# Hybrid encoder layer: v's second half as one 512-column panel, the backward scan's products on VectorE, the third chunk's attention factors behind the merge

## The chip, the cores and the metric

The kernel runs on one core of one Trainium2 chip. The metric is the device time of one execution in microseconds (us). Engines are named as in the profile: PE (TensorE, matmuls), PEld (its weight loads), DVE (VectorE), ACT (ScalarE), POOL (GpSimd) and SP (SyncE), whose queue issues the kernel's loads and stores. L12 is line 12 of the kernel.

## The reference

One encoder layer, in float32, over a prompt of 512 tokens and a sample of 1024 tokens, 1024 channels each. Both go through the same weights:

```python
h = rmsnorm(x, norm_pre_mix) @ w_in          # q, k, v, z, xBC, dt, gates
att = diff_attention(q, k, v, lam, rel_bias) # 8 heads of 2 x 64, v of 128
att = rmsnorm(att, subln_w) * (1 - LAM_INIT) # per head, over its 128 channels
ssm = ssd_scan(forward) + ssd_scan(backward) # 16 heads of 64, chunks of 128
m = gate_a * (att @ w_proj_attn) + gate_s * (ssm @ w_proj_ssm)
x = x + rmsnorm(m @ w_out, norm_post_mix)
y = x + rmsnorm(swiglu(rmsnorm(x, norm_pre_ffn)), norm_post_ffn)
```

(Names are shortened here; the bodies matter only as far as told below.) The attention's bias comes from a table of 32 distance buckets for each head. The scan keeps, for every chunk of 128 tokens and each of two groups, a state of 128 x 512 that is multiplied by a decay and to which a product of b with the weighted x is added; the backward scan does this from the last chunk to the first.

## The kernel before

**Products.** Each float32 operand is split into a high and a low part (`split`: a cast, then a subtraction), and each product is three matmuls (L169, L170, L171). All 1536 tokens are held as `hT`, in three chunks of 512 columns. A weight panel is 1024 rows by 256 columns: two raw pieces `wraw` of 512 KB are loaded (L156), cast to `whi` by ACT (L137) and subtracted to `wlo` by DVE (L138). `wraw`, `whi` and `wlo` have two buffers each, so one panel can be prepared while the other is used.

**Order.** The program is recorded in the order in which it is written; a scheduler then sets one fixed order for every engine. Each engine runs its own order from first to last and waits where an operand or a buffer isn't ready. So does SP, whose order holds all transfers.

**v.** The first 512 columns of v are made in the loop that makes `hT`. The second 512 are made by `proj_tm` (called at L494) in two panels of 256 columns. For each, six pairs of 128-token tiles share one PSUM bank: 48 matmuls of 256 columns, then one DVE copy of 128x2x256 (L376) and one store to `v_d` (L377).

**The bias table.** Ahead of that, in a pool named `pre2`, four matmuls (`fb_ps`, L478) pick the bias for 2048 distances and 8 heads; ACT copies them to `fb` (L479), and a store (L480) puts `fb` into `f_d`. Then `skew(h)` (L485) copies, for each head, the row of `f_d` 128 times into `sk_d`, each row one element further: one transfer of 1 MB for each head, from memory to memory. `skew` names a DVE copy of v behind which the scheduler should put it; it is a hint on order, and the transfer doesn't wait for that copy. The attention loads `tb` from `sk_d` (L225).

**The backward scan** (L693 to L707) runs over the chunks from last to first and two groups, prompt and sample apart. In a step, PE makes `yo_ps` from the old state (L703), DVE makes `yb` from it (L705) and it is stored; `state_step` (L675) makes `xw` from x on POOL (L679), PE makes `st_ps` (L681), POOL multiplies the old state by `dec` (L686) and DVE adds `st_ps` (L687). The first state of a sequence is copied by DVE (L684), and its last chunk ends without a new state. PE's matmuls of the z projection stand between these steps. The forward scan calls `state_step` too.

**The heads and what follows.** A head's output `av` (128 channels by 512 tokens) is copied by ACT (L323) and stored to `att_d` (L324). `mean_square` squares `av` in place (L327), and PE sums it (`ms`, L330). When all heads of a chunk are done, `att_scale(c)` makes the factors of 8 heads x 512 tokens (`zq`, `msq`, `att_r`, some 16 small DVE operations to L342), transposes them (`rt`, L344) and stores them to `r_d` (L347). `att(c)` later loads, for each head, the rows of `att_d` (L352) and the factors from `r_d` (L353), multiplies (L354) and splits them into `big`. `merge(c)` projects these and makes the gated sum, `out_proj` multiplies it by w_out, `norms` does the two RMSNorms around the residual and transposes the result. Their order in the text is att(1), merge(1), norms(0), att(2), out_proj of the first sample chunk, merge(2), norms(1).

Of the kernel before, what the change touches and what calls it, by code (L numbers as in the profile page):

```python
# [18 lines left out]
P = 128  # L19
# [59 lines left out]
def hybrid_trunk_kernel(ctx: ExitStack, tc: tile.TileContext, a: dict, y_prompt, y_sample):  # L79
# [55 lines left out]
    def split(hi, lo, raw, eng=None):  # L135
        if eng == "act_dve":
            S.copy(hi, raw)  # L137
            V.tensor_sub(lo, raw, f(hi))  # L138
        elif eng == "pool_dve":
            G.tensor_scalar(hi, raw, 1.0, 0.0, op0=ALU.mult, op1=ALU.add)  # L140
            V.tensor_sub(lo, raw, f(hi))
        elif eng == "act_pool":
            S.copy(hi, raw)
            G.tensor_sub(lo, raw, f(hi))
        else:
            G.tensor_scalar(hi, raw, 1.0, 0.0, op0=ALU.mult, op1=ALU.add)
            G.tensor_sub(lo, raw, f(hi))
# [120 lines left out]
    def attention(base, SL, h, got, pend, zq, msq, qk, pp, at, qr, s_ps, t_ps, o_ps):  # L268
        nkb = SL // P
        tb = got["tb"]  # L270
        qh, ql, km = zip(got[0], got[1])
        v_h = at.tile([P, nkb, P], F32R, tag="vh", name="vh", bufs=1)
        v_l = at.tile([P, nkb, P], F32R, tag="vl", name="vl", bufs=1)
        raw = staged(qr, [P, nkb, P], (None, v_d[base:base + SL, h * P:(h + 1) * P].rearrange("(b p) e -> p b e", p=P)))
        split(v_h[:], v_l[:], raw[:])
        for qc in range(SL // 512):
            ops = o_ps.tile([P, 512], F32, tag="o", name="o")
            for q2 in range(2):
                aT = [at.tile([P, 2, 4, 256], F32R, tag=f"aT{b0}", name="aT", bufs=2 - b0 // 4)
                      for b0 in range(0, nkb, 4)]  # L280
                for u in range(2):
                    if pend and (q2, u) == ((0, 1) if qc and h == 7 else PU):
                        pend.pop()()
                        if qc and h == 7:
                            att_scale(1, zq[0], msq[0], ap, t_ps, "t")
                    qt = qc * 4 + q2 * 2 + u
                    qs = slice(qt * P, (qt + 1) * P)
                    off = P * (nkb - 1 - qt)
                    nm = pp.tile([P, 2], F32, tag="nm", name="nm")
                    zs = pp.tile([P, 2], F32, tag="zs", name="zs")  # L290
                    z0 = zq[qc][:, h, qt % 4:qt % 4 + 1]
                    pm = []
                    for m in range(2):
                        sps = s_ps.tile([P, SL], F32, tag="s", name="s")
                        for kc in range(0, SL, 512):
                            ks = slice(kc, kc + 512)
                            TE.matmul(sps[:, ks], qh[m][:, qs], km[m][:, ks], start=True, stop=False)
                            TE.matmul(sps[:, ks], ql[m][:, qs], km[m][:, ks], start=False, stop=True)  # L298
                        pt = pp.tile([P, SL], F32, tag=f"p{m}", name="pt", bufs=3)
                        V.tensor_tensor_reduce(out=pt[:], in0=sps[:], in1=tb[:, off:off + SL], scale=-1.0,  # L300
                                               scalar=3.0e38, op0=ALU.add, op1=ALU.min,
                                               accum_out=nm[:, m:m + 1])
                        S.activation(out=pt, in_=pt, func=AF.Exp, bias=nm[:, m:m + 1], scale=-1.0,  # L303
                                     accum_out=(z0, zs[:, 0:1])[m])
                        pm.append(pt)
                    V.reciprocal(zs[:, 0:1], zs[:, 0:1])
                    V.scalar_tensor_tensor(zs[:, 1:2], zs[:, 0:1], z0, neglam, op0=ALU.mult, op1=ALU.mult)
                    last_add.append(V.scalar_tensor_tensor(pm[0], pm[1], zs[:, 1:2], pm[0], op0=ALU.mult, op1=ALU.add))
                    for b0 in range(0, nkb, 4):
                        ps = t_ps.tile([P, 4, P], F32, tag="t", name="t")  # L310
                        for j in range(4):
                            TE.transpose(ps[:, j, :], pm[0][:, (b0 + j) * P:(b0 + j + 1) * P], ident)
                        us = slice(u * P, (u + 1) * P)
                        ab = aT[b0 // 4]
                        S.copy(ab[:, 0, :, us], ps)
                        V.tensor_sub(ab[:, 1, :, us], ps, f(ab[:, 0, :, us]))
                    if u == 0:
                        yield
                gemm(ops[:, q2 * 256:q2 * 256 + 256],
                     [(v_h[:, b, :], v_l[:, b, :], aT[b // 4][:, 0, b % 4, :], aT[b // 4][:, 1, b % 4, :]) for b in range(nkb)])  # L320
                yield
            av = pp.tile([P, 512], F32, tag="av", name="av", bufs=1)
            S.copy(av, ops)  # L323
            store(out=att_d[h * P:(h + 1) * P, base + qc * 512:base + qc * 512 + 512], in_=av)  # L324

            def mean_square(av=av, qc=qc):
                S.activation(out=av, in_=av, func=AF.Square)  # L327
                ps = t_ps.tile([P, 4, P], F32, tag="t", name="ms")
                for j in range(4):
                    TE.matmul(ps[:, 0, j:j + 1], av[:, j * P:(j + 1) * P], onec, start=True, stop=True)  # L330
                V.tensor_copy(msq[qc][:, h], ps[:, 0, 0:4])
            pend.append(mean_square)

    def att_scale(c, zq, msq, pool, psp, ptag):

# [25 lines left out]
    with ExitStack() as ph1:  # L361
# [12 lines left out]
        def evac_v(p0, t, ps):  # L374
            so = st0.tile([P, 2, 256], F32, tag="st0", name="st")
            done = V.tensor_copy(so, ps)  # L376
            store(out=v_d[t * P:(t + 2) * P, p0:p0 + 256].rearrange("(j p) n -> p j n", p=P), in_=so)  # L377
            return done
# [49 lines left out]
        def proj_tm(col0, ncol, evac, eng="act_dve", start=0):  # L428
            for p0 in range(start, ncol, 256):
                w = split_panel(w_in[:, col0 + p0:col0 + p0 + 256], eng=eng)  # L430
                for t in range(0, NT, 2):
                    ps = acc.tile([P, 2, 256], F32, tag="acc", name="acc")
                    for u in range(2):
                        tt = t + u
                        gemm_tm(ps[:, u, :], w, hT[tt // 4], slice((tt % 4) * P, (tt % 4 + 1) * P))
                    evac(p0, t, ps)
# [45 lines left out]
        def skew(h, after):  # L482
            dst = sk_d[h]
            with tc.issue_after(after.ins):
                store(out=bass.AP(tensor=dst.tensor, offset=dst.offset, ap=[[SKP + 1, P], [1, 2048]]),  # L485
                      in_=f_d[h:h + 1].broadcast_to([P, 2048]))

        def evac_v_skew(p0, t, ps):
            done = evac_v(p0, t, ps)
            n = (p0 - 512) // 256 * 6 + t // 2  # L490
            if n < 8:
                skew(n, done)

        proj_tm(V0, D, evac_v_skew, start=512)  # L494
        pools = [es.enter_context(tc.tile_pool(name="p" + n, bufs=b, reuse_waits="tile")) for n, b in (
            ("qk", 1), ("pp", 2), ("at", 1), ("qr", 2))]
        pools += [es.enter_context(tc.tile_pool(name="p" + n, bufs=b, space=PSUM, reuse_waits="tile")) for n, b in (
# [168 lines left out]
        def hb(tl, c, d_, g):  # L666
            return tl[:, c, d_ * 16 + g * 8:d_ * 16 + g * 8 + 8].unsqueeze(2).broadcast_to([P, 8, 64])

        def h3(ap):
            return ap.rearrange("p (h e) -> p h e", e=64)  # L670
# [4 lines left out]
        def state_step(c, d_, g, x_g, b_g, old, last):  # L675
            if last:
                return None
            xw = sc.tile([P, 512], F32, tag="xw", name="xw")
            G.tensor_mul(h3(xw[:]), h3(x_g), hb(wst, c, d_, g))  # L679
            ps = ssp.tile([P, 512], F32, tag="ssp", name="st_ps")  # L680
            TE.matmul(ps, b_g, xw, start=True, stop=True)  # L681
            new = sc.tile([P, 512], F32, tag=f"s{g}", name="state")
            if old is None:
                V.tensor_copy(new, ps)  # L684
            else:
                G.tensor_mul(h3(new[:]), h3(old[:]), hb(dec, c, d_, g))  # L686
                V.tensor_add(new, new, ps)  # L687
            return new

# [113 lines left out]
    with ExitStack() as ph2:  # L803
# [36 lines left out]
        def side_work():  # L840
# [49 lines left out]
        side = side_work()  # L890
        run(heads(512, 1024, range(8), pend, zq, msq, qk, pp, at, qr, s_ps, t_ps, o_ps),
            side, RATIO)
        pend.pop()()
        att_scale(2, zq[1], msq[1], ap, t_ps, "t")
        for _ in side:
            pass

# [1 line left out]
    with ExitStack() as ph3:  # L899
# [153 lines left out]
        with ExitStack() as ph3a:  # L1053
# [53 lines left out]
            for j, mt in enumerate(t0[0]):  # L1107
                load(out=mt, in_=mo_d[j * P:(j + 1) * P, :])
            m1 = merge(1, aT1)
            norms(0, t0)  # L1110
            aT2 = att(2)
            t1 = out_proj(m1)
# [130 lines left out]
```

## Time and profile before

| | us |
|---|---|
| median of 3 runs | 3193.4 (3191.82 to 3199.23) |
| profiled execution | 3186.2 |
| its span | 3184.4 |
| PE busy | 3029.6 |
| DVE busy | 1835.1 |
| ACT busy | 1260.8 |
| POOL busy | 651.3 |

The profile is of one execution. Busy times are sums over the span, so a high share says that an engine is seldom free, and not which stage is bound by it. Times on the trace are counted from the start of the span. On them the stages that the change touches stand here: v's second half from 101.7 to 175, the backward scan from 834 to 930, and the last head of the attention at 1864, behind which the first merge ends at about 1942 and the out projection after it at about 2004. The mean granted clock of PE is 0.98.

### The profile page before, as it was taken

What the parts mean: (1) busy time and instruction counts of PE and PEld (TensorE: products, weight loads), DVE (VectorE), ACT (ScalarE), POOL (GpSimd) and SP (SyncE); (2) the same over time, 40 slices, a digit from 0 to 9 for tenths busy, and PEclk for the clock granted to TensorE, in tenths of its full rate; (3) what the DMA queues carried; (4) which work ended last, traced back from release to release, by engine and by line L of the source; (5) the groups of instructions that cost most, each with busy time, mean ns of one, the idle gap of its engine ahead of it and who ended that gap; (6) DMA issues with size and microseconds to landing.
All of it is one profiled execution on the core that took longest, in us unless ns stands there. A gap on an engine that the chain in (4) does not pass through costs nothing. (4 is left out here: it accounts for less than half of the span.)

```text
span 3184.4 us, 44184 instructions
## 1 busy us (share of the span) xinstructions
PE 3029.6 (95%) x16668; PEld 2664.2 (84%) x16668; DVE 1835.1 (58%) x2974; ACT 1260.8 (40%) x2305; POOL 651.3 (20%) x508
## 2 busy tenths in 40 slices
PE   7999999999999999999998978978999999989998
PEld 7988887888887778788887867878999899978887
DVE  5214444455328995387877955686666766632444
ACT  4103333333303333366666734453333333332443
POOL 0001111000233442243232100023333433300000
PEclk9999999999999999999999989988999999999999
DMA  4633333223554445765544156644333333363454
GB/s 149 195 100 112 110 103 110 62 74 107 161 163 146 145 137 156 217 182 160 181 135 148 64 194 216 198 153 139 98 103 101 100 98 101 105 203 97 125 164 132
DMA packets 444238, 433.64 MB, mean 136 GB/s; under 512 B 25536, under 2 KB 360865, under 8 KB 442913
## 3 DMA queue, kind: packets, MB, share of 16 engines
q1 hardware_dynamic: 444025, 430.82, 43.5%
q8 instruction: 131, 2.15, 0.3%
q14 instruction: 82, 0.67, 0.1%
HBM read 316.58 MB, written 122.54 MB: 138 GB/s over the span
## 5 line engine op out<-in xcount | busy, mean ns | idle before, releaser
L169 PE MATMUL acc<-hT,whi 128*128 128x512 f32 x1056 | 421.3, 399 | 2.9 <-ACT st L455 2.9
L170 PE MATMUL acc<-hT,whi 128*128 128x512 f32 x1056 | 416.6, 395 | 0.0
L171 PE MATMUL acc<-hT,wlo 128*128 128x512 f32 x672 | 262.2, 390 | 0.0
L169 PEld LDWEIGHTS acc<-hT,whi 128*128 128x128 f32 x1056 | 198.9, 188 | 48.9 <-issue 5.5
L303 ACT ACTIVATE pt<-pt,nm 128x1024 f32<-128x1024 f32 (+1 forms) x192 | 193.1, 1007 | 116.2 <-DVE nm L300 113.1
L170 PEld LDWEIGHTS acc<-hT,whi 128*128 128x128 f32 x1056 | 199.0, 188 | 42.6 <-issue 3.6
L300 DVE CUSTOM_DVE_ANT_0 pt<-s,tb 128x1024 f32<-128x1024 f32 (+1 forms) x192 | 197.3, 1041 | 53.2 <-PE s L298 40.1
L169 PE MATMUL acc<-whi,hT 128*128 128x256 f32 x768 | 225.0, 293 | 0.6 <-ACT hT L208 0.4
L171 PE MATMUL acc<-whi,hT 128*128 128x256 f32 x768 | 224.7, 293 | 0.4 <-DVE hT L209 0.3
L170 PE MATMUL acc<-wlo,hT 128*128 128x256 f32 x768 | 224.0, 292 | 0.0
L169 PE MATMUL d<-dhi,fh 128*128 128x512 f32 x528 | 206.5, 391 | 5.9 <-ACT fh L137 5.9
L171 PE MATMUL d<-dhi,fl 128*128 128x512 f32 x528 | 206.3, 391 | 4.2 <-DVE fl L138 4.2
L170 PE MATMUL d<-dlo,fh 128*128 128x512 f32 x528 | 206.4, 391 | 0.0
L137 ACT CAST whi<-wraw 128x1024 fp32r<-128x1024 f32 (+1 forms) x115 | 115.8, 1036 | 216.4 <-PE acc L170 82.8
L138 DVE TENSOR_TENSOR fl<-raw,fh 128x896 fp32r<-128x896 f32 (+1 forms) x70 | 79.4, 1136 | 193.1 <-ACT fh L137 193.1
L169 PE MATMUL mm<-op,wy 128*128 128x384 f32 x528 | 178.9, 339 | 6.6 <-ACT op L137 5.0
L236 POOL TENSOR_TENSOR ql<-raw,qh 128x512 fp32r<-128x512 f32 x48 | 66.0, 1389 | 576.2 <-ACT qh L233 533.1
L170 PE MATMUL mm<-op,wy 128*128 128x384 f32 x528 | 178.6, 338 | 0.2 <-DVE op L138 0.2
L171 PE MATMUL mm<-op,wy 128*128 128x384 f32 x528 | 178.4, 338 | 0.0
L138 DVE TENSOR_TENSOR wlo<-wraw,whi 128x1024 fp32r<-128x1024 f32 x80 | 96.2, 1227 | 121.2 <-ACT whi L137 110.7
L169 PEld LDWEIGHTS acc<-whi,hT 128*128 128x128 f32 x768 | 148.0, 193 | 10.9 <-issue 9.4
L171 PE MATMUL acc<-hT,whi 128*128 128x512 f32 x384 | 155.5, 405 | 0.0
(375 smaller groups left out, 8191.1 us busy)
## 6 DMA issues: line engine op xcount, KB each, us to landing
wraw<-in_w_in_dram SPq DMA_DIRECT2D x60, 512.0 KB
wraw<-in_w_gate_up_dram SPq DMA_DIRECT2D x92, 256.0 KB
raw<-ff_d SPq DMA_DIRECT2D x46, 448.0 KB
wr<-in_w_gate_up_dram SPq DMA_DIRECT2D x80, 256.0 KB
ff_d<-c SPq DMA_DIRECT2D x88, 192.0 KB
g_d<-st SPq DMA_DIRECT2D x48, 256.0 KB
xg<-xs_d SPq DMA_DIRECT2D x48, 256.0 KB
gt<-g_d SPq DMA_DIRECT2D x48, 256.0 KB
```

The source lines that it names most:

```text
L137: S.copy(hi, raw)
L138: V.tensor_sub(lo, raw, f(hi))
L169: TE.matmul(ps, ah, bh, start=(i == 0), stop=False)
L170: TE.matmul(ps, ah, bl, start=False, stop=False)
L171: TE.matmul(ps, al, bh, start=False, stop=(i == n - 1))
L236: G.tensor_sub(q_l[:, s_], q_r[:, s_], f(q_h[:, s_]))
L300: V.tensor_tensor_reduce(out=pt[:], in0=sps[:], in1=tb[:, off:off + SL], scale=-1.0, scalar=3.0e38, op0=ALU.add, op1=ALU.min, accum_out=nm ...
L303: S.activation(out=pt, in_=pt, func=AF.Exp, bias=nm[:, m:m + 1], scale=-1.0, accum_out=(z0, zs[:, 0:1])[m])
```

## The change

Three edits. First, v's second half is one panel of 512 columns, in a pool `vp` with one buffer for each of `vhi` and `vlo`. Four raw pieces (two column halves by two row halves) are loaded and split into it; twelve tiles of 128 tokens follow, each 24 matmuls of 512 columns, a DVE copy and a store of 128x512. A skew is named behind each of the first eight. Second, in the backward scan `xw` and the state's product with `dec` go to DVE. Third, the last head's `mean_square` and the third chunk's `att_scale` are taken from the end of the heads; behind merge(1), the last head's rows are loaded again from `att_d`, and both are done there.

```diff
+            if not (qc and h == 7):
+                pend.append(lambda av=av, qc=qc: mean_square(av, msq[qc][:, h], t_ps, "t"))
...
-        def evac_v_skew(p0, t, ps):
-            done = evac_v(p0, t, ps)
-            n = (p0 - 512) // 256 * 6 + t // 2
-            if n < 8:
-                skew(n, done)
-
-        proj_tm(V0, D, evac_v_skew, start=512)
+        with tc.tile_pool(name="vp", bufs=1, reuse_waits="tile") as vp:
+            vhi, vlo = [vp.tile([P, KB, 512], F32R, name=n) for n in ("vhi", "vlo")]
+            for cs in (slice(0, 256), slice(256, 512)):
+                for ks in (slice(0, 4), slice(4, 8)):
+                    raw = rp.tile([P, 4, 256], F32, tag="wraw", name="wraw")
+                    load(out=raw, in_=w_in[:, V0 + 512 + cs.start:V0 + 512 + cs.stop].rearrange("(a p) c -> p a c", p=P)[:, ks])
+                    split(vhi[:, ks, cs], vlo[:, ks, cs], raw[:], "act_dve")
+            for t in range(NT):
+                ps = acc.tile([P, 512], F32, tag="acc", name="acc")
+                gemm_tm(ps, (vhi, vlo), hT[t // 4], slice(t % 4 * P, (t % 4 + 1) * P))
+                so = st0.tile([P, 512], F32, tag="st0", name="st")
+                done = V.tensor_copy(so, ps)
+                store(out=v_d[t * P:(t + 1) * P, 512:D], in_=so)
+                if t < 8:
+                    skew(t, done)
...
-            G.tensor_mul(h3(xw[:]), h3(x_g), hb(wst, c, d_, g))
+            E = V if d_ else G
+            E.tensor_mul(h3(xw[:]), h3(x_g), hb(wst, c, d_, g))
...
-                G.tensor_mul(h3(new[:]), h3(old[:]), hb(dec, c, d_, g))
+                E.tensor_mul(h3(new[:]), h3(old[:]), hb(dec, c, d_, g))
...
-        pend.pop()()
-        att_scale(2, zq[1], msq[1], ap, t_ps, "t")
...
             m1 = merge(1, aT1)
+            av = wk.tile([P, 512], F32, tag="araw", name="av", bufs=3)
+            load(out=av, in_=att_d[7 * P:8 * P, 1024:T])
+            mean_square(av, msq[1][:, 7], tr_ps, "tr")
+            att_scale(2, zq[1], msq[1], ap, tr_ps, "tr")
             norms(0, t0)
             aT2 = att(2)
```

`mean_square` is otherwise the same code, made a function beside `att_scale`.

What stands on SP behind v's first half, in the program before (a row is a line of the kernel, the transfer with its destination and source, and the destination's size; "x2" is two of them):

```order
L377 DMA v_d<-st 128x2x256 x2
L156 DMA wraw<-in_w_in_dram 128x4x256 x2
L480 DMA f_d<-fb 8x2048
L485 DMA sk_d<-f_d 128x2048 x2
L377 DMA v_d<-st 128x2x256
L485 DMA sk_d<-f_d 128x2048 x6
L225 DMA tb<-sk_d 128x896
```

And at the same place on SP in the changed program, where L495 is the load of v's raw pieces (its first two stand further up) and L156 here loads the K projection's:

```order
L482 DMA f_d<-fb 8x2048
L487 DMA sk_d<-f_d 128x2048 x4
L495 DMA wraw<-in_w_in_dram 128x4x256
L487 DMA sk_d<-f_d 128x2048
L495 DMA wraw<-in_w_in_dram 128x4x256
L487 DMA sk_d<-f_d 128x2048 x3
L156 DMA wraw<-in_w_in_dram 128x4x256 x2
L502 DMA v_d<-st 128x512 x2
```

The third raw piece stands behind the store of `f_d` and four skews, the fourth behind a fifth skew; before, both panels' pieces stood ahead of `f_d`. In the changed program the first cast into `vhi` also waits for the store of `f_d`, since `vp` lies in memory that held `fb`.

On PE, at the same place, the changed program has:

```order
L171 MATMUL acc<-whi,hT_693 128x256
L480 MATMUL fb_ps<-oh,rb 8x512 x4
L169 MATMUL acc<-vhi,hT_116 128x512 x2
L170 MATMUL acc<-vlo,hT_116 128x512
L171 MATMUL acc<-vhi,hT_116 128x512
```

All four bucket matmuls stand ahead of v's first one (there were two, then 27 of v, one, 3 of v, one), and v's first needs a cast of the third piece, since its 512 columns reach over both column halves.

The DVE order at the beginning of the backward scan, before:

```order
L684 COPY state<-st_ps 128x512
L739 CAST sl<-slr 120x256
L705 TENSOR_TENSOR yb<-yo_ps,eac 128x512
L687 TENSOR_TENSOR state<-state,st_ps 128x512
L705 TENSOR_TENSOR yb<-yo_ps,eac 128x512
L687 TENSOR_TENSOR state<-state,st_ps 128x512
```

and in the changed program, with L690 the product for `xw`, L697 the one with `dec`, L716 `yb` and L698 the addition:

```order
L697 TENSOR_TENSOR state<-state,dec 128x512
L716 TENSOR_TENSOR yb<-yo_ps,eac 128x512
L698 TENSOR_TENSOR state<-state,st_ps 128x512
L690 TENSOR_TENSOR xw<-xg,wst 128x512
L697 TENSOR_TENSOR state<-state,dec 128x512
L716 TENSOR_TENSOR yb<-yo_ps,eac 128x512
```

Both products now stand in line with `yb` and the addition.

Last, PE behind the heads. Before, the sums of the last head and the transposition of the factors stood between the last head and the merge:

```order
L171 MATMUL o<-aT,vl 128x256
L330 MATMUL ms<-onec,av 128x1 x4
L344 MATMUL rt<-ident,att_r 32x128
L169 MATMUL mm<-big,whi 128x512
L170 MATMUL mm<-big,whi 128x512
```

In the changed program the sums stand ahead of the merge's eighth head, and the transposition at its end, in front of the out projection:

```order
L171 MATMUL mm<-big,wlo 128x512
L346 MATMUL rt<-ident,att_r 32x128
L1105 MATMUL tr_ps<-ident,mt 128x128 x4
L169 MATMUL mm<-whi,big 128x256
L170 MATMUL mm<-wlo,big 128x256
```

The transposes `tr_ps` of norms(0), of which several stood among the merge's last two heads, now stand all behind the merge, between the out projection's matmuls. On SP the loads of att(2) stood among the merge's transfers and now stand behind the store of the third chunk's factors, at the merge's end.

More of the change, by code (lines that the diff above doesn't have):

```diff
@@ L324, in attention, with mean_square @@
             store(out=att_d[h * P:(h + 1) * P, base + qc * 512:base + qc * 512 + 512], in_=av)
[L326 to L332, printed above, removed]
+            if not (qc and h == 7):
+                pend.append(lambda av=av, qc=qc: mean_square(av, msq[qc][:, h], t_ps, "t"))
+    def mean_square(av, out, psp, ptag):
+        S.activation(out=av, in_=av, func=AF.Square)
+        ps = psp.tile([P, 512], F32, tag=ptag, name="ms")
+        for j in range(4):
+            TE.matmul(ps[:, j:j + 1], av[:, j * P:(j + 1) * P], onec, start=True, stop=True)
+        V.tensor_copy(out, ps[:, 0:4])
     def att_scale(c, zq, msq, pool, psp, ptag):
```

## The prediction

> **What bounds the kernel now.** I read the page's busy shares first, then the windows by stage, then, only for the three stages that the change touches, the waits, the timeline and the DMA issues.
>
> ```profile
> PE 3029.6 (95%) x16668; PEld 2664.2 (84%) x16668; DVE 1835.1 (58%) x2974; ACT 1260.8 (40%) x2305; POOL 651.3 (20%) x508
> 85.00:175.00 90.00, 90.00 (x724) 86.27 (x724) 16.77 (x21) 8.09 (x10) 0.00 (x0) 1.00 0.57 179
> 175.00:640.00 465.00, 460.18 (x2221) 382.72 (x2220) 196.93 (x373) 144.11 (x270) 64.45 (x67) 1.00 0.32 102
> 800.00:960.00 160.00, 156.00 (x1046) 133.51 (x1045) 46.99 (x73) 32.06 (x45) 49.83 (x45) 0.99 0.54 167
> 1864.00:1942.00 78.00, 54.74 (x219) 42.84 (x219) 53.39 (x108) 26.57 (x46) 0.00 (x0) 0.85 0.78 257
> 1942.00:2004.00 62.00, 52.30 (x404) 51.22 (x403) 21.99 (x27) 29.98 (x72) 0.00 (x0) 0.89 0.55 183
> 2004.00:2048.00 44.00, 44.00 (x195) 36.14 (x194) 34.34 (x68) 21.28 (x39) 0.00 (x0) 1.00 0.70 233
> ```
>
> The page's line shows PE busy 95% of the span. In a window's row, the stretch and its length come first, then the busy time of PE, PEld, DVE, ACT and POOL, then the granted clock, the DMA share and GB/s. PE is full while v is made (85 to 175) and nearly full beside the backward scan (800 to 960). It is loose only behind the heads: 23.3 us idle of 78 in the first merge, 9.7 of 62 in the out projection after it, at a clock of 0.85 and 0.89. So an edit counts by what it does to PE's stream: shorter work counts at once in the first two stages, a removed wait counts only in the third, and a new wait counts anywhere.
>
> **Part 1: v's second half. Its work.**
>
> ```profile
> 140.06 0.28 PE L170 MATMUL acc<-wlo,hT 128*128 128x256 f32 x1
> 140.18 0.28 PE L171 MATMUL acc<-whi,hT 128*128 128x256 f32 x1
> 190.19 0.39 PE L170 MATMUL acc<-hT,whi 128*128 128x512 f32 x1
> 190.42 0.39 PE L171 MATMUL acc<-hT,wlo 128*128 128x512 f32 x1
> ```
>
> The timeline gives start and duration. Start to start, the 256-column matmul costs 0.12 us; 512 columns, which the K projection already uses, cost 0.227 (more digits: 0.2267 over the steps around it). The half takes 576 of the first, 69.1 us, and will take 288 of the second, 65.3. Work alone: 3.8 us less. Evacuations fall from 24 pieces of 256 columns to 12 of 512, on a DVE that is busy 16.8 of 90 us: nothing.
>
> On that saving a page speaks lower: the Trainium skill, "TensorE: Matmul & The Clock Gate", section "Back-to-back issue gap", gives a warm gap of N/2.4 + 2.5 ns for an isolated matmul, so by it, an estimate, 109 and 216 ns here and a saving of 0.8 us, not 3.8. The rows differ from it (120 and 227 ns), and the measurement decides.
>
> **Its start.** The larger cost is in the queue. The order of the changed program puts all four bucket matmuls ahead of the panel, and its first matmul needs columns from the third raw piece; that piece's load stands on SP behind the store of f_d and four skew copies, and the fourth behind a fifth. Before, the weights were cast ahead.
>
> ```profile
> 101.73 1.99 ACT L137 CAST whi<-wraw 128x1024 fp32r<-128x1024 f32 x2 [9.51 <-PE acc L171]
> 107.87 0.57 ACT L479 COPY fb<-fb_ps 8x512 f32<-8x512 f32 x1 [3.20 <-PE fb_ps L478]
> 101.68 0.69 DVE L376 COPY st<-acc 128x512 f32<-128x512 f32 x1 [5.06 <-PE acc L171]
> 102.81 2.36 DVE L138 TENSOR_TENSOR wlo<-wraw,whi 128x1024 fp32r<-128x1024 f32 x2 [0.43 <-ACT whi L137]
> 111.70 0.69 DVE L376 COPY st<-acc 128x512 f32<-128x512 f32 x1 [6.54 <-PE acc L171]
> 109.97 0.29 SPq L480 DMA_DIRECT2D f_d<-fb  x1
> 112.47 1.20 SPq L485 DMA_DIRECT2D sk_d<-f_d  x2
> 114.75 4.06 SPq L485 DMA_DIRECT2D sk_d<-f_d  x6
> 123.70 0.36 SPq L377 DMA_DIRECT2D v_d<-st  x1
> 145.34 0.69 DVE L376 COPY st<-acc 128x512 f32<-128x512 f32 x1 [2.53 <-DMA v_d<-st]
> sk_d<-f_d SPq DMA_DIRECT2D x8, 1024.0 KB
> 135.00:145.00 10.00, 10.00 (x86) 10.00 (x85) 1.66 (x2) 1.99 (x2) 0.00 (x0) 1.00 1.00 318
> ```
>
> What the reader is to see: eight skews of 1 MB were issued within 7 us of 112.5, and fill the DMA (share 1.0) until 145. The store of v issued at 123.70, behind them, had not released its buffer until 145.34, where a DVE copy waited for it: 21.6 us for 256 KB. So SP's transfers go in the order in which they were issued. A skew costs between 3.3 us (1 MB at 318 GB/s) and 4.1 ((145.3 - 112.5)/8); this pace was harmless before, because no weights stood behind it.
>
> Step by step. The first half ends at 101.7. The bucket matmuls take (111.70 - 101.68) - 48 x 0.12 = 4.3 us, so PE is out of work at 106. The last fb copy ends at 106.5, and f_d lands 2.5 us after its issue (109.97 to 112.47), at about 109.3. The new panel's memory lies over that of fb, so the first cast waits for this landing: cast 1.0 us (1.99/2), subtraction 1.2 (2.36/2), done at 111.5. This frees the raw buffer; the third load is issued at 112, behind four skews issued from 109.4. Those occupy 13.3 to 16.4 us. With 512 KB at 318 GB/s (1.6 us) the piece lands between 124.3 and 127.4, and I take 126.5, nearer to the upper end, since the landing was late in the 21.6 us row too. Its cast ends at 127.5: PE idles 21.5 us. Twelve matmuls (2.7 us) later it needs the fourth piece, which comes a skew and a load later (4.9 to 5.7): 2.5 us more. I add 1.5 us for the clock: behind the 8.49 us gap at 1881 (rows under part 3) the matmuls of 512 columns started 0.43 us apart (1881.75, 1882.18), and some 4 us later 0.23 apart again (1885.37, 1885.60). The half ends at 127.5 + 2.5 + 65.3 + 1.5 = 196.8 instead of 175: **+21.8, taken as +21**. The K projection stands behind it, and nothing fills the hole, since the order has no other PE work there.
>
> Bounds: if loads overtook the skews, the third piece would land 1.6 us of transfer and 2.5 of latency behind 112, at 116; v ends then near 184, **+8**. If every skew costs 4.1 us and the clock 2: **+24**.
>
> **Part 2: the backward scan.** Twenty products xw and sixteen of the state with dec go from POOL to DVE.
>
> ```profile
> L679 POOL TENSOR_TENSOR xw<-xg,wst 128x512 f32<-128x512 f32 x21 | 22.5, 1072 | 126.5 <-DMA xg<-xs_d 92.2 <-PE st_ps L681 34.3
> L705 DVE TENSOR_TENSOR yb<-yo_ps,eac 128x512 f32<-128x512 f32 x18 | 12.4, 691 | 26.6 <-DMA yb_d<-yb 16.2 <-PE yo_ps L703 10.4
> PE yo_ps L703 <- DVE yb L705: 2.3, 1, 2.3
> PE st_ps L681 <- POOL xw L679: 0.7, 1, 0.7
> ```
>
> By the group on DVE of the same shape, 36 x 0.69 = 25 us move to an engine that was busy 47 of 160 us. The waits of PE in 800 to 960 name the scan with 3.0 us in all; that is the most that a quicker product can give. Against it: the products now stand in DVE's one queue behind yb, which has waited 16.2 us for its store, so a wait that was nobody's becomes one of the state chain. That is some 0.9 us for each of its 18 instructions. I bound this at +4 and take **-1**, because PE runs the z projection between scan steps, and order and cadence are set by that.
>
> **Part 3: the third chunk's factors.**
>
> ```profile
> 1870.11 0.63 ACT L327 ACTIVATE av<-av 128x512 f32<-128x512 f32 x1 [5.45 <-DMA att_d<-av]
> 1870.79 1.87 PE L330 MATMUL ms<-onec,av 128*128 128x1 f32 x8 [6.75 <-ACT av L327]
> 1881.15 0.37 PE L344 MATMUL rt<-ident,att_r 128*32 128x128 f32 x1 [8.49 <-DVE att_r L342]
> 1881.75 0.63 PE L170 MATMUL mm<-big,whi 128*128 128x512 f32 x1
> 1882.18 0.63 PE L171 MATMUL mm<-big,wlo 128*128 128x512 f32 x1
> 1885.37 0.39 PE L170 MATMUL mm<-big,whi 128*128 128x512 f32 x1
> 1885.60 0.39 PE L171 MATMUL mm<-big,wlo 128*128 128x512 f32 x1
> 1881.87 0.32 SPq L347 DMA_DIRECT2D r_d<-rt  x1
> 1904.71 0.62 ACT L137 CAST big<-araw 128x512 fp32r<-128x512 f32 x1 [1.12 <-DVE araw L354]
> 1908.74 0.62 ACT L137 CAST big<-araw 128x512 fp32r<-128x512 f32 x1 [3.41 <-DVE araw L354]
> 1913.24 0.62 ACT L137 CAST big<-araw 128x512 fp32r<-128x512 f32 x1 [3.89 <-DVE araw L354]
> 1947.33 0.58 PE L169 MATMUL mm<-whi,big 128*128 128x256 f32 x1 [3.15 <-ACT big L930]
> ```
>
> Two waits of 6.75 and 8.49 us go from the head of the merge. They are not worth 15.2: the merge's eight heads come in by load, scale and cast, 4.3 us apart ((1913.24 - 1904.71)/2), while one head's 12 matmuls take 2.7, and the last head's cast at 1913 sets what follows. Without the wait for rt, whose store also held SP's queue until 1882, the third and later heads move up by some 3 us, and the reload of av takes part of that back: the merge ends about 2 us earlier.
>
> The larger part is the out projection. The transposes of norms move there from the merge's tail and, with rt, stand where PE now waits (9.7 us by the window, the 3.15 of the row at 1947 among them). Most of it can close, and the clock of 0.89 rises with them: I take 9, together **-11**; all of it, 9.7 + 2 + 2.3 for clock, is **-14**. What is late next is the second att: its rows now wait for r_d at the merge's end, then seven heads at 4.3 us behind a first one that needs two transfers, a store and a load (2.5 us each by f_d's, 5.45 by att_d's) and 2 us of scale and cast: 37 to 43 us against an out projection of about 53. It just fits; if it slips past, part 3 falls to **-3** or, at a pace of 6, to 0.
>
> **Sum.** +21 - 1 - 11 = +9 against the profiled execution (3186.2 us, span 3184.4). The stages between only shift: in 175 to 640 PE's busy time is nearly the whole stretch. The median of the runs shown, 3193.4, is 7.2 above the profiled one; I put the difference on it: **3202 us**.
>
> **The rivals.**
> - *Loads pass the skews.* If the third and fourth pieces aren't held, part 1 is +8, and the sum 8 - 1 - 11 = -4 (3189), or at best 8 - 3 - 14 = -9 (3184). For it: two loads are small beside the skews. Against it: the 21.6 us of the v store. This is the faster side, and it decides from a third load that lands before 120.
> - *The second att paces the next merge.* Part 3 gives 0 to -3; the sum is +17 to +20 (3212). For it: 4.3 us a head leaves 10 to 16 us of room, and DVE and ACT have more to do there. Against it: the merge in 2004 to 2048 ran full.
> - *The waits behind the heads close fully and the skews are quick.* Part 1 at +18, part 3 at -14, and the merge another 5 us earlier, since its heads no longer share the queue with rt: -2 to +3 (3194). For it: PE's idle of 23.3 us in the merge is there to be taken. Against it: casts 4.3 us apart.
>
> **How the numbers follow.** The forecast has 0.5, loads passing 0.2, the pacing att 0.15, full closing 0.15. About 0.2%, 6.4 us, is what a measurement of this kernel can tell from no change. Of the forecast's 0.5, 0.38 lie above +6.4 and 0.12 within; the pacing case is slower; loads passing splits 0.09 faster, 0.11 same; full closing is 0.12 same and 0.03 faster. Slower 0.53, same 0.35, faster 0.12. The range takes the passing case down to below its middle and the pacing case whole: 3186 to 3214.
>
> **What would show it.** Right: an idle of some 20 us on PE at about 106, ended by a cast of vhi; a third piece's load with a landing time above 12 us; v ending near 197; no ms or rt wait after 1885 (shifted by 21); an out projection under 56 us. Wrong: a first vhi matmul before 120, waits on DVE xw or state beside the z projection, or PE waiting for big in the second merge.

## The result, and the profile after

The changed kernel took 3240.68 us (median of 4 runs, 3236.6 to 3247.85) against 3192.61 us before (3187.23 to 3199.23). The ratio is 1.0148, with a 95% interval of 1.0128 to 1.0167: **47 us slower, between 41 and 53**. A second set gave 1.0118 (1.0099 to 1.0137), 38 us. Forecast were +9 us and a range that ended at 3214.

The page of the profiled execution (3236.6 us) and its windows; columns as before (stretch, length, then busy PE, PEld, DVE, ACT, POOL, granted clock, DMA share, GB/s). The first two windows are the same stretches of time as before, the last two the same stages, some 42 us later:

```profile
PE 3035.1 (94%) x16380; PEld 2654.2 (82%) x16380; DVE 1857.0 (57%) x3010; ACT 1260.7 (39%) x2305; POOL 616.4 (19%) x472
...
85.00:175.00 90.00, 67.14 (x344) 55.24 (x344) 17.31 (x20) 10.58 (x12) 0.00 (x0) 0.85 0.55 173
800.00:960.00 160.00, 154.07 (x1059) 133.61 (x1058) 78.75 (x119) 36.86 (x49) 8.22 (x6) 0.99 0.52 164
1905.00:1984.00 79.00, 53.69 (x208) 40.85 (x207) 49.92 (x101) 24.73 (x43) 0.00 (x0) 0.87 0.71 235
1984.00:2041.00 57.00, 51.08 (x417) 50.11 (x416) 26.06 (x34) 29.65 (x70) 0.00 (x0) 0.97 0.66 209
```

The reader is to see three things. PE is no longer full where v is made: 22.9 us idle of 90, where there were none. In the scan, POOL has given its work (49.8 to 8.2 us) to DVE (47.0 to 78.8), and PE's idle is 5.9 instead of 4.0 of 160. The merge (1905 to 1984) has no less idle than before, 25.3 us in a window 1 us longer, to 23.3; the out projection behind it has 5.9, not 9.7.

What happened ahead of the panel, on ACT, SP and PE in the timeline (start, duration, and in brackets the idle time before and what ended it):

```profile
108.63 1.99 ACT L137 CAST vhi<-wraw 128x1024 fp32r<-128x1024 f32 x2 [2.69 <-DMA f_d<-fb]
127.04 1.04 ACT L137 CAST vhi<-wraw 128x1024 fp32r<-128x1024 f32 x1 [16.43 <-DMA wraw<-in_w_in_dram]
130.93 1.04 ACT L137 CAST vhi<-wraw 128x1024 fp32r<-128x1024 f32 x1 [2.84 <-DMA wraw<-in_w_in_dram]
...
108.39 2.70 SPq L487 DMA_DIRECT2D sk_d<-f_d  x4
111.19 0.77 SPq L495 DMA_DIRECT2D wraw<-in_w_in_dram  x1
...
128.14 1.22 PE L169 MATMUL acc<-vhi,hT 128*128 128x512 f32 x2 [22.82 <-ACT vhi L137]
```

This is the forecast almost number for number: first cast behind the landing of `f_d` at 108.6 (forecast 109.3), third load issued at 111.2 behind four skews (112), its cast at 127.0 (126.5), and PE idle for 22.8 us (21.5).

To find the rest, the start of each DVE and ACT instruction was taken from two traces, and the difference set against its time before. Medians of that shift at a few places, in us, against the one profiled execution of before:

| time before | changed | panel alone | delay of PE | scan alone | factors alone |
|---|---|---|---|---|---|
| 200 | 20.9 | 20.3 | 20.9 | 0.7 | 2.0 |
| 570 | 25.4 | 24.8 | 26.6 | 3.6 | 3.3 |
| 1000 | 27.3 | 26.2 | 27.0 | 3.8 | 3.4 |
| 1100 | 31.1 | 30.3 | 30.6 | 4.7 | 4.2 |
| 1650 | 42.7 | 38.7 | 38.8 | 13.7 | 11.2 |
| 1860 | 42.0 | 36.2 | 35.8 | 13.1 | 9.9 |
| 2190 | 41.4 | 42.1 | 36.9 | 15.6 | 10.8 |
| 2500 | 51.1 | 43.0 | 34.6 | 15.2 | 20.1 |
| 3170 | 50.3 | 43.0 | 35.3 | 14.5 | 19.6 |

A caution: the profiled execution of before, 3186.2 us, is one of its fastest (medians of its sets lie between 3192 and 3200), so a shift of up to some 15 us at the end can mean nothing: the scan alone ends at +14.5 in its profile and has a ratio of 0.9998. Sizes are therefore taken from the ratios over many runs, and the table only tells where to look. There are 21 us at v, some steps between 540 and 1700, and about 9 in gate_up, from 2190 to 2500, in the kernels with the moved factors.

### The profile page after: what moved, and what is told of

Same layout as the page of the kernel before. It is cut to its first block, busy times and chain, and to the rows that moved or that the text cites. A ratio compares the mean times of both kernels' runs of the same rounds, so it can differ in the third digit from the quotient of the medians.

```text
span 3234.8 us, 43568 instructions
## 1 busy us (share of the span) xinstructions
PE 3035.1 (94%) x16380; PEld 2654.2 (82%) x16380; DVE 1857.0 (57%) x3010; ACT 1260.7 (39%) x2305; POOL 616.4 (19%) x472
## 4 chain that ended last, share of the span: by engine, by line
PE 64%; DMA 14%; DVE 9%; issue 5%; ACT 4%; POOL 3%; SPq 1%; ACTq 0%; POOLq 0%; DVEq 0%
PE acc L169 9%; PE acc L171 9%; PE acc L170 9%; PE mm L169 4%; PE mm L170 4%; PE mm L171 4%; PE d L171 4%; PE d L170 4%; PE d L169 4%; DMA araw<-r_d 2%; DMA wraw<-in_w_gate_up_dram 1%; DMA raw<-k_d 1%; PE s L297 1%; PE t L312 1%; PE s L298 1%
## 5 line engine op out<-in xcount | busy, mean ns | idle before, releaser
L169 PE MATMUL mm<-op,wy 128*128 128x384 f32 x528 | 178.9, 339 | 11.2 <-ACT op L137 8.9
L171 PE MATMUL acc<-whi,hT 128*128 128x256 f32 x576 | 170.7, 297 | 0.4 <-DVE hT L209 0.3
L169 PE MATMUL acc<-whi,hT 128*128 128x256 f32 x576 | 170.2, 296 | 0.6 <-ACT hT L208 0.4
L170 PE MATMUL acc<-wlo,hT 128*128 128x256 f32 x576 | 169.0, 294 | 0.0
L137 ACT CAST fh<-raw 128x896 fp32r<-128x896 f32 (+1 forms) x70 | 68.8, 984 | 213.3 <-PE d L170 204.0
L297 PE MATMUL s<-km,qh 128*128 128x512 f32 x320 | 133.3, 416 | 15.3 <-DVE nm L300 8.4
```

Source lines behind the costliest of these rows:

```text
L169: TE.matmul(ps, ah, bh, start=(i == 0), stop=False)
L170: TE.matmul(ps, ah, bl, start=False, stop=False)
L171: TE.matmul(ps, al, bh, start=False, stop=(i == n - 1))
```

## The experiments

Unless said otherwise, a ratio is that of many runs to runs of the kernel before on the same chip, in brackets its 95% interval, and us are worked out on the median of before.

### Each part alone

The first three are the hunks of the diff one by one, the fourth is the change without the panel.

> Only v's second half is one panel; the scan and the third chunk's factors are as before. Theory A (the stall in front of the panel is paid once, and what follows only shifts): about 21 us over the kernel before, PE idle some 22 us ahead of the first vhi matmul, and the same 21 us still there at the sample's heads and at the end. Theory B (a shift of 21 us disturbs later stages, whose transfers and casts no longer meet PE as before): 35 to 45 us, with 10 more from the sample's heads and 8 more from gate_up. Theory C (what later stages lost varies from execution to execution and belongs to no edit): a shift at the end of 21, plus or minus 10, that differs between executions.

> Only the backward scan's products are on VectorE. Theory A (cost in its own place): +2 in the backward scan and +5 in the forward scan, whose loads the scheduler ordered anew, so +7 at the end. Theory as predicted: -1, between -3 and +4. Theory B (knock-on): +15 to +25, with the sample's heads losing 10 as well.

> Only the last head's sum and the third chunk's factors are moved behind the merge. As predicted: -11 (-14 to 0), from the out projection. Theory A (by the trace of the changed kernel, whose merge gained about 3 us): -2 to -4. Theory B (the new order of the merge also puts gate_up out of step): -3 + 8 = +5.

> All but the panel. Theory A: +7 - 3 = +4. Theory B for the panel alone (the shift by v disturbs the rest): about +4 here too, with the sample's heads and gate_up as before. If the sample's heads and gate_up lose 18 us here as well, the cause lies in the scan or the factors: +20 or more.

| | ratio | us |
|---|---|---|
| panel alone | 1.0101 (1.0085 to 1.0116) | +32 |
| scan alone | 0.9998 (0.9988 to 1.0008) | -1 |
| factors alone | 1.0014 (1.0002 to 1.0025) | +4 |
| scan and factors | 1.0011 (0.9995 to 1.0028) | +4 |

The scan can't be told from nothing, as predicted. The factors lose a little (1 to 8 us) where -11 was forecast. The panel has its 20.3 us at v and loses some 12 more behind it: theory A falls for the panel. Theory C falls too, since its four runs lie within 7 us. Theory B is nearest, though the panel alone (27 to 37 us) lies mostly below its 35 to 45, and the 8 us that it put down to gate_up aren't there (42.1 at 2190, 43.0 at 2500).

### Is it the delay, the queue, or the panel?

`pe_delay` is the kernel before with idle work for PE in front of v's second half, its sum used by nothing:

```diff
+        with tc.tile_pool(name="dly", bufs=1, space=PSUM) as dly:
+            ps = dly.tile([P, 512], F32, name="dly_ps")
+            for i in range(92):
+                TE.matmul(ps, hT[0][0][:, 0, 0:P], hT[0][0][:, 1, :], start=True, stop=True)
         proj_tm(V0, D, evac_v_skew, start=512)
```

> The kernel before, with 92 more matmuls of 512 columns (20.9 us at 0.227) ahead of v's second half; their sum is used by nothing. PE is late by that and busy all the while, and nearly all engines keep their order. Theory A (a shift is only a shift): +21, within the measurement's interval. Theory B (later stages lose some 10 us more when PE comes late): +30 to +33, as the panel alone.

`panel_skews_behind` is the panel alone with the skews ordered behind the fourth piece on SP:

```diff
-                    load(out=raw, in_=w_in[...])
+                    piece = load(out=raw, in_=w_in[...])
...
-            with tc.issue_after(after.ins):
+            with tc.issue_after(piece.ins):
```

> The panel alone, with the eight skew copies put behind the load of the fourth raw piece in SP's order; the memory of the panel still lies over the bias table's, and the order of the later stages is that of the kernel before. Theory 'the queue holds the pieces': the third piece lands near 116, PE idles 11 to 13 us in place of 22, and the whole is +7 to +10. Theory 'the pieces are late for another reason' (the cast that waits for the bias table's store): PE idles 20 us or more again. Theory B on later stages: +17 to +20; theory A: +7 to +10.

`panel_prepared_early` moves the pool `vp`, the loads and the splits ahead of the pool of the bias table; the tile loop stays behind it.

> The panel alone, with its memory apart from the bias table's and its four pieces loaded and split ahead of the table, so that neither skew nor store stands before them. By the width of the matmuls alone: -4 (69.1 to 65.3 us), PE idle less than 1 us there. If the order of gate_up, which changes by a few instructions with this edit, matters: up to +4.

`factors_before_merge` has the factors alone, with the four lines of the reload written ahead of `m1 = merge(1, aT1)`.

> The third chunk's factors alone, from reloaded rows, but written ahead of merge(1) in place of behind it; the scheduler then orders gate_up's first stretch otherwise than in the changed kernel. Theory 'gate_up is out of step by the new order at its start': gate_up loses less than 3 us (8 to 10 in the three profiles that have the factors behind the merge), and the whole is -4 to 0. Theory 'the reload itself costs': +4 as with the factors behind the merge.

| | at v, by the trace | ratio | us | behind v |
|---|---|---|---|---|
| delay of PE | +20.9 | 1.0099 (1.0085 to 1.0112) | +32 | +11 |
| panel, skews behind | +10.0 | 1.0070 (1.0057 to 1.0082) | +22 | +12 |
| panel, prepared early | -3.8 | 1.0026 (1.0015 to 1.0038) | +8 | +12 |
| factors before the merge | | 1.0005 (0.9992 to 1.0018) | +2 | |

Of `panel_skews_behind`, the casts into the panel on ACT and PE's wait:

```profile
108.94 1.99 ACT L137 CAST vhi<-wraw 128x1024 fp32r<-128x1024 f32 x2 [2.70 <-DMA f_d<-fb]
114.92 1.04 ACT L137 CAST vhi<-wraw 128x1024 fp32r<-128x1024 f32 x1 [3.99 <-DMA wraw<-in_w_in_dram]
...
PE acc L169 <- ACT vhi L137: 10.4, 1, 10.4
```

The queue theory holds, for about half of the stall: with the skews behind, PE's idle fell from 22.8 to 10.4 us. The other 10.4 us are the chain that begins with the store of `f_d`: the first casts still wait for it, and only the subtractions behind them free the raw buffers for the third piece. With the panel prepared early, which takes both away, the idle was gone, and the 512-column matmuls then gained the 3.8 us that were worked out for them. But all three lose the same 11 to 12 us behind v, whether PE comes 21 us late or 4 us early. So it isn't the delay as such, and theory B as it was put falls too.

What these kernels share is that PE's count of instructions ahead of the later stages has changed, by -288 or +92 matmuls. (They share one small change of order too, told below with the prompt's factors.) The kernels were then compared at one place of the forward scan in which all engines of the delayed kernel ran in lockstep with before, 27.04 us late, up to one load. Over the same 10 us of work, the DMA queues and SP's waits. First the panel alone, in its second profile (`v_only_again` below); a row of a queue gives packets, MB and the share of the DMA engines, a row of SP's waits the sum, how many and the longest:

```profile
q8 instruction: 1, 0.02, 0.6%
...
SPq L757 <- DMA bg<-bt_d: 5.5, 2, 4.5
...
1040.91 0.80 PE L689 MATMUL st_ps<-xw,bg 128*128 128x512 f32 x1 [2.25 <-POOL xw L687]
...
1040.00:1050.00 10.00, 9.09 (x40) 6.91 (x41) 6.71 (x12) 1.10 (x3) 5.23 (x4) 0.83 0.48 147
```

and the kernel before, where that stretch has packets of the data queue alone:

```profile
q1 hardware_dynamic: 2032, 1.92, 61.4%
...
SPq L749 <- DMA bg<-bt_d: 3.9, 2, 3.1
...
1011.46 0.70 PE L681 MATMUL st_ps<-xw,bg 128*128 128x512 f32 x1 [0.62 <-POOL xw L679]
```

Queue q8 carries one packet of 16 KB there: PE's own program. That it is PE's is inferred from the counts: there are 131 such packets over the kernel before (2.15 MB, with 16668 matmuls and as many weight loads), 129 with 288 matmuls fewer and 132 with 92 more, and from one to the next PE begins 256 instructions (median of the kernel before). Here one falls between the loads of the scan; SP waits 5.5 us for `bg` instead of 3.9, the next load of x is issued 1.5 us later on the kernel's own time, PE waits 2.25 us instead of 0.62 for the product of it, and then the clock falls too (0.83 in these 10 us). The Trainium skill, "Runtime: NRT & Kernel Launch", section "Instruction fetch mechanics", says that the engines' instruction stores are refilled in blocks of 16 KiB, 256 instructions, over a queue of their own; the counts agree. It calls the cost mostly hidden. In the stretch shown no wait of PE is put down to a fetch, and the data load beside it is what comes late.

### Putting the fetches back

By the 256 instructions from packet to packet, 288 matmuls with their weight loads are 576 instructions, two blocks and 64 more. The 92 matmuls of the delay are 184, one block less 72. So the panel, which takes 576 away, and the delay, which adds 184, move the later fetches to nearly the same places of the program, 64 and 72 instructions from where they were, and that is how kernels so unlike can lose the same. Thirty-two small matmuls, used by nothing, give these 64 back:

```diff
+            with tc.tile_pool(name="dly", bufs=1, space=PSUM) as dly:
+                ps = dly.tile([P, 512], F32, name="dly_ps")
+                for i in range(32):
+                    TE.matmul(ps[:, 0:64], hT[0][0][:, 0, 0:P], hT[0][0][:, 1, 0:64], start=True, stop=True)
             for t in range(NT):
```

> The changed kernel with 32 more matmuls of 64 columns, used by nothing, ahead of the panel's first matmul, where PE waits anyway; every engine's order is otherwise that of the changed kernel. In the profiles, the fetches of PE's instructions (16 KB, 256 instructions each) stand at other places of the program in the kernels with the panel than in those without; 288 matmuls fewer are 576 instructions with their weight loads, 64 more than two whole fetches, and 32 matmuls give these 64 back. Theory 'fetches that meet the loads': the fetches stand again where they were before, and 8 to 12 us of the 47 go: +35 to +39. Theory 'order and shift': nothing goes, +47.

> The panel alone, prepared early, with the same 32 small matmuls (some 2 us of PE). Theory 'fetches': the 12 us that the panel prepared early lost behind v go, so -3.8 + 2 = -2, plus 0 to 3 for the sums that stand later in front of the factors' transposition (3.7 in place of 2.3 us): -2 to +2. Theory 'order and shift': +8 + 2 = +10.

The next two add 92 or 128 matmuls of 64 columns to the kernel before, at the place of the delay.

> The kernel before with 92 matmuls of 64 columns, used by nothing, ahead of v's second half: as many instructions as in the delay of 20.9 us, and the same orders, but only some 5 us of PE. Theory 'fetches': it is the number of instructions that counts, 5 + 11 = +14 to +18. Theory 'a late PE disturbs what follows': 5, and a quarter of 11: +6 to +8.

> The same with 128 matmuls of 64 columns, 256 instructions with their weight loads, so one whole fetch: the later fetches stand at the same places of the program as before. Theory 'fetches': +6 to +8 for the matmuls themselves and nothing behind, less than with 92. Theory 'order and shift': as 92 or more, in proportion.

| | at v, by the trace | ratio | us | behind v |
|---|---|---|---|---|
| changed, padded | +21.4 | 1.0098 (1.0082 to 1.0115) | +31 | +10 |
| early, padded | -1.5 | 1.0018 (1.0007 to 1.0030) | +6 | +7 |
| before, 92 small | +18.7 | 1.0082 (1.0065 to 1.0100) | +26 | +8 |
| before, 128 small | +23.7 | 1.0083 (1.0068 to 1.0099) | +27 | +3 |

All four point the way of the fetches, and none settles it. The changed kernel padded is 16 us below the first set's 47, but no set of the changed kernel stood beside it. The early panel padded came to +6 (2 to 10) where -2 to +2 was expected. The small matmuls were mis-sized: 92 of them started between 113.0 and 129.7, 0.18 us apart instead of the 0.05 reckoned with, at a granted clock of 0.76 in 100 to 130, so they were nearly as long a delay as the first. What is left behind v is 3 us with one whole block, 8 with 92, but the intervals are about 5 us wide to each side, and the orders weren't quite the same: the kernel with 92 has the delay's small change of order, and the one with 128 moved a few instructions of a head. So pairs with the same orders were run side by side.

> The panel alone, as in the first set, again, as the partner of the next run: +32, of which 20 in front of the panel and some 12 behind it.

> The panel alone with 32 matmuls of 64 columns, used by nothing, in PE's idle time ahead of the panel; every engine's order is otherwise that of its partner. Theory 'fetches': 5 to 10 us less than its partner. Theory 'order and shift': the same as its partner, within 4 us.

> The panel alone with the skews behind the fourth piece, again, as the partner of the next run: +22, of which 10 in front of the panel and some 12 behind it.

> The same with the 32 small matmuls in PE's idle time, and otherwise the same orders. Theory 'fetches': 5 to 10 us less than its partner. Theory 'order and shift': the same as its partner, within 4 us.

> The changed kernel itself, beside the next run on the same chip. The parts add up to about 37 (panel 32, scan and factors 3.5 to 4, less than 1 apart); the first set gave 47. Theory 'the parts add': +37 to +42. Theory 'together they cost more': +47 again.

> The changed kernel with the 32 small matmuls in PE's idle time, its partner with the same orders. Theory 'fetches': 9 to 10 us less than its partner, as in the other two pairs. If they cost more in the whole kernel: 16 less.

| pair | as it was | with 32 matmuls more | less |
|---|---|---|---|
| panel alone | 3229.39 (3225.13 to 3237.10) | 3220.10 (3217.73 to 3229.91) | 9.3 |
| panel, skews behind | 3221.97 (3215.21 to 3226.44) | 3211.35 (3208.07 to 3218.78) | 10.6 |
| changed kernel | 3235.18 (3228.23 to 3240.16) | 3227.92 (3218.38 to 3234.46) | 7.3 |

Medians in us, with the lowest and highest run. Work was added, every order stayed, and each kernel became 7 to 11 us faster. The ranges of the partners overlap; by the means the differences are 8.2, 8.3 and 7.7 us, each give or take 5 to 8. They don't arise at v, where the partners' profiles lie within 0.7 us of each other. The place in the forward scan agrees. The panel alone with the 32 matmuls has no fetch in that stretch, and the same rows read (the window of the clock is 2 us earlier, as the kernel is there):

```profile
SPq L761 <- DMA bg<-bt_d: 4.3, 2, 3.4
...
1039.27 0.70 PE L693 MATMUL st_ps<-xw,bg 128*128 128x512 f32 x1 [1.12 <-POOL xw L691]
...
1038.00:1048.00 10.00, 8.88 (x47) 6.90 (x47) 7.54 (x14) 2.75 (x9) 5.41 (x4) 1.00 0.48 147
```

The 20 profiles of all kernels fall into two groups. Take a fetch between 900 and 1600 us, count PE's instructions from it to the program's end, and leave out whole blocks of 256: the rest is 200 to 209 (medians) in 11 of them (the kernel before, those without the panel, the padded ones and the 128 small ones) and 129 to 141 in 9 (the panel's unpadded, the delay and the 92 small ones). The 9 have a fetch in the 10 us, the 11 have none:

| profiles | SP's wait for `bg` | the shift grows, from 990 to 1100 of before's time |
|---|---|---|
| 9 with a fetch | 4.7 to 6.1, one 4.0 | 1.5 to 4.2 |
| 11 without | 3.9 to 4.5, one 4.9 | 0 to 0.9, one 3.0 |

So one meeting costs some 3 us here, more than the load was late by. The single 4.0 is `changed_again`, the 4.9 and the 3.0 are both the changed kernel padded, which lost time here without a fetch: something else can do it too. How much each of the 129 fetches costs wasn't measured one by one; the 8 us are the sum over all stages, and that they all arise as at this one place is inferred.

As to the sum: panel 32, scan and factors 4, together 36; the whole gave 47 (41 to 53) and then 38 (32 to 44). The parts add up to the second set. The first lies 11 us above them, and why the two sets differ stays open. A hint stands in the next section: their two profiles differ by 8 us in gate_up (1.6 us lost in the second set's, 9.7 in the first's), but these are one run of each.

### The factors and gate_up

From 2190 to 2470, in gate_up's loop, PE never waited before. With the factors behind the merge it does. The groups over nearly the same part of the loop, of `factors_only` and then of `factors_before_merge` (columns: count, busy us and mean ns, idle before and what ended it):

```profile
L169 PE MATMUL mm<-op,wlo 128*128 128x384 f32 x136 | 46.2, 340 | 3.8 <-DVE c L1044 3.8
L169 PEld LDWEIGHTS mm<-op,wlo 128*128 128x128 f32 x136 | 25.5, 188 | 5.5 <-DVE c L1044 5.4
```

```profile
L169 PE MATMUL mm<-op,wlo 128*128 128x384 f32 x152 | 51.1, 336 | 0.0
L169 PEld LDWEIGHTS mm<-op,wlo 128*128 128x128 f32 x152 | 28.6, 188 | 0.0
```

The scheduler gave the first blocks of gate_up another order on DVE, ACT and SP when the factors were moved, and, but for a few swaps, none further on. From 2190 to 2500 of before's time, five of six profiles with the factors behind the merge lose 8 to 10 us; the sixth, of `changed_again`, loses 1.6, with the same order. With the factors written ahead of the merge, and again another order, 1.3 are lost. The waits for `c` in the five come to 2.6 to 4.2 us, so they name less than half of what is lost. By these six, the new order makes the loop liable to fall out of step, and doesn't always do it. Why the sixth didn't, and where the rest goes, stays open.

## Why the prediction was wrong, point by point

- **The stall in front of the panel** was right in mechanism and size: forecast +21, measured 20.9 at v. The skews behind took 12.4 us of it away, early preparation all of it. The saving by wide matmuls, 3.8 us, was right too: 3.8. Two small terms were off and cancelled: the 2.5 us for the fourth piece never came as a wait, since PE's first matmuls ran slowly (0.43 us apart up to 132.6), and the clock cost 2.5 us and not 1.5 (the panel took 67.8 us from its first matmul, where 65.3 were its work); PE's idle was 22.8 and not 21.5.
- **The scan** came out as forecast, but -1 (-4 to +3) can't be told from 0. One of the prediction's own signs of being wrong did come: in the changed kernel PE waited 1.5 us for `xw` on DVE. It is too small to be seen in the time: the scan alone has a shift of 3.6 us at 570 and 3.8 at 1000.
- **"The stages between only shift"** is one of the two steps that failed, with some 12 us put at nothing. The reason given was that PE is full in 175 to 640. By the table most of the shift's growth lies behind that, between 1000 and 1700, where PE does wait for what small loads bring, and the position of the fetches of PE's program wasn't in the sum at all. They follow the count of PE's instructions, so an edit that removes 288 matmuls moves every later fetch. By the pairs this is 7 to 11 us. A smaller piece is the prompt's factors: in every kernel with the panel, in the delay and with the 92 small matmuls, the scheduler put four `ms` matmuls behind six others, and PE's wait for the transposition grew from 2.27 to 3.70 us:

```profile
580.62 0.37 PE L346 MATMUL rt<-ident,att_r 128*32 128x128 f32 x1 [3.70 <-DVE att_r L344]
```

- **The third chunk's factors** are the other step that failed, and the larger miss: forecast at -11, they came to +4, 15 us off. The merge was to end 2 us earlier; by the first and last matmuls it ended 78.4 us after the heads' last matmul, where it was 77.5. The wait for `rt` (8.49) went and that for `ms` fell from 6.75 to 1.3, and waits for the heads' rows, 23.3 us of them where there were 6.2, stand in their place:

```profile
1914.57 0.79 PE L169 MATMUL mm<-big,whi 128*128 128x512 f32 x1 [8.57 <-ACT big L137]
...
PE mm L169 <- ACT big L137: 23.3, 7, 8.6
```

  That removing 15 us there is worth little was seen, but not that it is worth nothing: the second head's cast comes 19.7 us after the heads' last matmul, 20.3 before. The out projection gained 5.6 us (56.5 instead of 62.1), not 9; the mechanism was right, the size 1.6 times too large. And gate_up, which the prediction doesn't speak of, lost 8 to 10 us and so gave back more than that. The rival in which the second att paces the next merge didn't come: that merge ran in 43.7 us as before.
- The sum was +9, in which -11 was the only large gain. With the terms as measured, 21 + 12 - 1 + 4 = +36, it is near the second set's 38 and 11 below the first one's 47. The forecast had the sign, and the time lay outside its range.

No version tried beats the kernel before. Nearest are the scan alone and the factors ahead of the merge, within the measurement, and the panel prepared early and padded, 6 us slower (2 to 10).

## What to carry to other kernels

Before a load is made the first thing that a full engine waits for, look at what stands ahead of it in its queue, and whose memory it takes: four copies of 1 MB and a store cost 23 us of PE for a gain of 4. Where small waits on loads set the pace, changing the number of instructions of an engine is an edit to all that comes after, even with every order kept, so test it with a padded twin before a cause is sought in the edit itself. A wait that is removed from the head of a chain is worth only what the next arrival allows.

## What the runs showed of the hardware

One fetch of 16 KB took 1.1 us on its DMA engine (median of the kernel before, 0.9 to 1.9), one every 23 us or so, and where it met the loads of the scan SP waited about 1 us longer and the kernel lost about 3. No wait of PE was put down to it in the stretch looked at. The scheduler is touchy in the same way: a few matmuls more at v changed the order of the heads far behind it in some variants and not in others, so a variant says something only when its order has been compared too. And a run of 64-column matmuls isn't cheap. They started 0.11 us apart at first, and 0.21 once the granted clock had fallen to 0.5, which it did 2.8 us into the 92 and 5 us into the 128; 92 matmuls of 512 columns, 0.227 apart, at the same place kept it at 1.0.
